# A decoder step on one core: the first norm, the last norm and two conditioning products are rearranged

## The chip, the core and the metric

One Trainium2 chip, one of its cores. The core has a matrix engine (TensorE, PE in the profile), a vector engine (VectorE, DVE), an activation engine (ScalarE, ACT), a general engine (GpSimd, POOL) and a sequencer that mostly issues transfers (SyncE, SP). Sixteen DMA engines carry all transfers. The metric is the device time of one execution in microseconds (us); lower is better. The inputs are float32; the kernel splits each large operand into a float32r high part and a float32r remainder ("hi" and "lo") and forms a product from three passes, so that it stays near float32.

## The reference

`x` is 1024 prompt rows and 8 x 8 sample rows of 1024 features, 1088 columns in the kernel's layout (features on partitions, 8 row blocks of 128 features). Cut to what the change touches:

```python
sh, sc, gt = ada_mod(c, w_ada_mix, b_ada_mix)        # silu(c) @ w + b, split in three
h = rms_norm(x, norm_mix) * (1 + sc) + sh            # the first norm
P = h @ w_in                                         # 34 column blocks of 128
...                                                  # RWKV-7 branch, pooling branch, merge
x = x + gt * (merged @ w_out)
sh, sc, gt = ada_mod(c, w_ada_mlp, b_ada_mlp)
h = rms_norm(x, norm_mlp) * (1 + sc) + sh
x = x + gt * (square(relu(h @ w_ff1)) @ w_ff2)
y = rms_norm(x, norm_final)                          # the last norm
```

`rms_norm` divides each row of `x` by the root of the mean of its squares. In the kernel's layout that mean runs across partitions.

## The kernel before, in words

**Order.** PE takes its instructions in the order of the program; the other engines' order is set by a scheduler from dependencies. Which piece of PE work comes next is decided while the program is written out: class `Pace` keeps a count of planned PE nanoseconds. A background generator (`back`) yields one product triple at a time; foreground generators yield either a number (planned nanoseconds until their next piece) or a condition. So a gap given in the code places a piece of work at a point of PE's order; if its data is late, PE stands still there.

**Start (`start`, L342 to L409).** Eight blocks `x` (544 KB each) are loaded over SP's queue, the sample columns once more as `smp` over ACT's queue (L350). Each block is squared on ACT (L362) and added up on DVE (L366). `stats` (L276) multiplies the sum with a column of ones, so that rows of `x` come to lie on partitions; root (L286), reciprocal (L287), a PE transpose of the broadcast result (L293) and a copy (L303) give `rb`, the reciprocal root on all partitions. The conditioning `silu(c) @ w_ada_mix` is done in parts of 1024 columns by `ada_part` (L239): four steps of two 512 KB tiles `aw`, PE work `wc<-aw,sT`, then a copy `asb` (L255), four small products that bring features back onto partitions (L259) and the bias (L263). Part 0 gives shift and scale of blocks 0 to 3, part 1 those of 4 to 7; part 2 (the gate) is done later in `ada_fill`. With them a block's row is made: `h` (L391, DVE), `hi` (L393, ACT), `lo` (L395, DVE), the sample columns by L386 to L388, L394 and L396.

**First products.** `phase1` (L1146) runs the column blocks J4 and J12 of `w_in` first, one row block of `h` at a time: for each of the eight rows, three column chunks of each of the two jobs, three passes each (18 products a row, 144 in all). Afterwards the other 32 jobs run, `weights` (L157) preparing each 128 x 512 half: load, `whi` on ACT (L167), `wlo` on DVE or POOL (L168).

**Middle (`phase2`, L1223).** Eight `or_job`s form the merged rows `t` (L1262, L1266 on POOL, hi and lo by L1269 and L1270), then `out_job(m, i)` multiplies them with `w_out`: eight `m` with two column chunks (i = 0), then eight with the third chunk (i = 1). The second conditioning, `ada` (L1238), runs beside them through `ada_part` with its tiles in the pool `hid`. Its first four tiles are passed through `behind` (L1233): POOL copies one column of the newest `t` at that point of the program into the tile, so that its load can't start before that `t` is there. The first step is placed 9000 + 6500 planned ns after job 4, the others 6500 apart.

**End.** `last` (L1401) multiplies the last group of `w_ff2` chunk by chunk over the column chunks `FCH` (L1506); `residual` (L1454, and L1457 with L1459 for sample columns) adds each block to `x`. `norm3` (L1422) follows a chunk behind: squares (L1431), sums (L1433), `stats` (L1436), `rms` (L1437), then eight rows out: one DVE instruction each (L1444), in the last chunk two of them on POOL and ACT (L1441, L1442), and a store on SP's queue (L1445).

Of the kernel before, what the change touches and what calls it, by code (L numbers as in the profile page):

```python
# [18 lines left out]
P = 128  # L19
# [98 lines left out]
class K:  # L118
# [38 lines left out]
    def weights(self, src):  # L157
# [10 lines left out]
        (nc.gpsimd if n % 2 and n >= self.solo else nc.vector).tensor_tensor(lo, raw, hi.bitcast(F32), op=ALU.subtract)  # L168
# [112 lines left out]
    def rms(self, po, col, blocks, out):  # L281
# [5 lines left out]
        nc.vector.reciprocal(r, r)  # L287
        yield 2000
        for i in range(0, k, 4):
            m = min(4, k - i)  # L290
            ps = self.ps("wc")
# [50 lines left out]
    def start(self, st, order):  # L342
# [4 lines left out]
        aw = lambda: st.tile([P, 1024], F32, tag="aw", bufs=8, name=self.nm("aw"))  # L347
        asb = st.tile([P, 512], F32, name="asb")
        smp = st.tile([P, 8, 64], F32, name="smp")
        nc.scalar.dma_start(smp, io["xT"][:, :, NPR:NT].rearrange("k p n -> p k n"))  # L350
        blocks = self.blocks(0, NT)
        po = self.ps("w")
        rt = self.cp.tile([P, 16], F32, tag="rt", bufs=2, name=self.nm("rt"))
        nc.scalar.activation(rt[:, 0:1], self.eps[:, 0:1], AF.Sqrt)
        xs = []
        t = None
        for kb in range(8):
            x = self.row(st, "x", 8)
            nc.sync.dma_start(x, io["xT"][kb])
            xs.append(x)  # L360
            sq = self.row(st, "sq", 3)
            nc.scalar.activation(sq, x, AF.Square)  # L362
            if t is None:
                t = sq
            else:
                nc.vector.tensor_tensor(t, t, sq, op=ALU.add)  # L366
        ws = []

        def load(i):
            for k in range(8):  # L370
                ws.append(aw())
                nc.sync.dma_start(ws[-1], io["w_ada_mix"][k, i])
# [3 lines left out]
        self.stats(po, t, blocks, True, True)  # L376
        rb = self.row(st, "rb", 1)
        pr, sa = slice(0, NPR), slice(NPR, NT)

        def part(i, gaps, turn):  # L380
            yield from self.ada_part("w_ada_mix", i, lambda: ws.pop(0), asb, self.am, "b_mix", (4 * i, 8 + 4 * i), gaps, turn)
            self.mod_scale(g, self.am, "norm_mix", 4 * i, 4 * i + 4)
            ks = slice(4 * i, 4 * i + 4)
            seq = lambda t: t[:, ks, 1:9].unsqueeze(3).to_broadcast([P, 4, 8, 8])
            s4 = smp[:, ks].rearrange("p k (q t) -> p k q t", t=TS)
            nc.vector.tensor_tensor(smp[:, ks], smp[:, ks], rb[:, sa].unsqueeze(1).to_broadcast([P, 4, 64]), op=ALU.mult)  # L386
            nc.vector.tensor_tensor(s4, s4, seq(g), op=ALU.mult)
            nc.vector.tensor_tensor(s4, s4, seq(self.am), op=ALU.add)  # L388
            for kb in range(4 * i, 4 * i + 4):
                x, h, hi, lo, sh = xs[kb], self.row(st, "h", 2)[:, pr], self.hh[kb], self.hl[kb], self.am[:, kb, 0:1]  # L390
                nc.vector.scalar_tensor_tensor(h, x[:, pr], g[:, kb, 0:1], rb[:, pr], op0=ALU.mult, op1=ALU.mult)  # L391

                nc.scalar.activation(hi[:, pr], h, AF.Identity, bias=sh)  # L393
                nc.scalar.activation(hi[:, sa], smp[:, kb], AF.Copy)  # L394
                nc.vector.scalar_tensor_tensor(lo[:, pr], h, sh, hi[:, pr].bitcast(F32), op0=ALU.add, op1=ALU.subtract)  # L395
                nc.vector.tensor_tensor(lo[:, sa], smp[:, kb], hi[:, sa].bitcast(F32), op=ALU.subtract)  # L396

        self.pace.run(iter(()), [part(0, (0, 3500, 0, 0), 1000), self.rms(po, 0, blocks, rb)])
        load(1)

        def rest():
            yield from part(1, (0, 0, 3000, 1500), 1500)
            self.done.add("h")
# [65 lines left out]
    def pool_cols(self, g):  # L469
# [4 lines left out]
        def begin():  # L474
# [3 lines left out]
            nc.sync.dma_start(ev[:, :, 0:15], self.io["spool"][:, g])  # L478
# [46 lines left out]
    def pools(self):  # L525
# [3 lines left out]
        for g in range(4):  # L529
            plw = self.pxp.tile([P, P], F32, tag="plw", bufs=1, name=self.nm("plw"))  # L530
            nc.sync.dma_start(plw, self.io["pool_w"][:, g * 128:(g + 1) * 128])
# [691 lines left out]
    def phase2(self):  # L1223
# [14 lines left out]
        def ada():  # L1238
# [183 lines left out]
        def norm3():  # L1422
            rb = T()
            for ci, (c0, n) in enumerate(FCH):
# [3 lines left out]
                for m in range(8):  # L1428
# [9 lines left out]
                for m in (7, 6, 0, 1, 2, 3, 4, 5):  # L1438
                    x = self.xr[m][:, c0:c0 + n]
                    if m > 5 and ci == 2:  # L1440
                        nc.gpsimd.tensor_tensor(x, x, rb[:, c0:c0 + n], op=ALU.mult)  # L1441
                        nc.scalar.activation(x, x, AF.Copy, scale=self.par("norm_final", m))  # L1442
                    else:
                        nc.vector.scalar_tensor_tensor(x, x, self.par("norm_final", m), rb[:, c0:c0 + n], op0=ALU.mult, op1=ALU.mult)  # L1444
                    nc.sync.dma_start(io["o_y"][m][:, c0:c0 + n], x)  # L1445
# [60 lines left out]
FCH = [(0, 448), (448, 384), (832, 256)]  # L1506
# [71 lines left out]
```

## Time and profile before

| what | value |
|---|---|
| time, median of 3 runs | 1757.21 us (1755.92 to 1760.8) |
| the profiled execution: its time / its span | 1759.32 us / 1757.5 us |
| mean granted clock of PE in it | 0.984 |
| PE busy | 1692.8 us, 96% of the span |
| DVE / ACT / POOL busy | 845.0 / 546.1 / 255.1 us |
| DMA | 179.61 MB, mean 102 GB/s |

Rows of the timeline read: start (us from the span's start), length, engine, line, operation, output <- inputs, shape, count, and in brackets how long the engine had stood still before it and what ended that. Rows of the waits read: the waiting engine and line, what it waited for, us in total, times, longest. Windows give a stretch, its length, the busy time and the instructions of PE, PEld, DVE, ACT and POOL, the granted PE clock, the busy share of the DMA engines and GB/s. The span leaves out 1.8 us of the profiled execution's time.

### The profile page before, as it was taken

How to read it: one execution, taken by the hardware profiler on the slowest of the kernel's cores; microseconds unless marked ns; L12 is line 12 of the kernel's file. 1: busy time of each engine (PE TensorE's matmuls, PEld its weight loads, DVE VectorE, ACT ScalarE, POOL GpSimd, SP SyncE). 2: the span in 40 equal slices, each digit the busy share in tenths (PEclk: the TensorE clock that was granted, in tenths of full speed). 3: DMA queues.
4: the chain of work that ended last, by engine and by line, in shares of the span. 5: the costliest groups of instructions: out<-in, count | busy, mean ns of one | idle time of the engine just before them, and what ended most of it. 6: DMA issues, size and time to landing. Idle time of an engine off the chain costs nothing.

```text
span 1757.5 us, 32572 instructions
## 1 busy us (share of the span) xinstructions
PE 1692.8 (96%) x13705; PEld 1583.7 (90%) x13705; DVE 845.0 (48%) x1540; ACT 546.1 (31%) x1100; POOL 255.1 (15%) x335
## 2 busy tenths in 40 slices
PE   5999999999999999999999999999999999999997
PEld 2989878887888798899798999999999999999997
DVE  5577465746573744335437633323333333324346
ACT  4443343343343433322225521213121212212132
POOL 0120110000000000005314411111111111111111
PEclk9999999989999999999999999999999999999998
DMA  8233314222413241847842311111111111111112
GB/s 336 82 128 118 125 65 135 85 81 94 147 41 129 80 137 57 314 168 276 299 151 85 136 45 49 43 44 47 43 46 45 43 49 43 43 49 43 43 43 103
DMA packets 80083, 179.61 MB, mean 102 GB/s; under 512 B 16480, under 2 KB 23136, under 8 KB 79936
## 3 DMA queue, kind: packets, MB, share of 16 engines
q1 hardware_dynamic: 72128, 156.66, 26.0%
q10 hardware_dynamic: 6512, 15.96, 2.7%
q0 software_dynamic: 1296, 4.90, 0.7%
q8 instruction: 108, 1.77, 0.4%
q14 instruction: 39, 0.32, 0.1%
HBM read 138.64 MB, written 38.84 MB: 101 GB/s over the span
## 4 chain that ended last, share of the span: by engine, by line
PE 86%; DMA 4%; DVE 4%; ACT 2%; issue 2%; POOL 1%; SPq 0%; DVEq 0%; ACTq 0%; POOLq 0%
PE mm L148 58%; PE w L148 24%; PE wc L148 4%; DMA t<-d_th 1%; DMA smp<-in_xT 1%; PE w L155 1%; POOL t L1266 1%; DMA aw<-in_w_ada_mix 1%; DMA wraw<-in_w_in 1%; DMA hid<-in_w_ada_mlp 0%; ACT whi L167 0%; DVE hx L1444 0%; DMA wraw<-in_w_ff 0%; POOL wlo L168 0%; DVE wlo L168 0%
## 5 line engine op out<-in xcount | busy, mean ns | idle before, releaser
L148 PE MATMUL mm<-hx,whi 128*128 128x362 f32 (+2 forms) x2608 | 683.1, 344 | 2.6 <-ACT px L465 2.0
L148 PEld LDWEIGHTS mm<-hx,whi 128*128 128x128 f32 x2608 | 458.8, 191 | 39.6 <-issue 20.4
L148 PE MATMUL mm<-hx,wlo 128*128 128x362 f32 (+3 forms) x1304 | 430.7, 330 | 1.8 <-DVE wlo L168 1.8
L167 ACT ACTIVATE whi<-wraw 128x512 fp32r<-128x512 f32 x246 | 155.1, 630 | 531.4 <-PE w L148 359.1
L148 PE MATMUL mm<-ma,whi 128*128 128x364 f32 (+1 forms) x1280 | 318.0, 330 | 0.2 <-ACT whi L167 0.2
L148 PEld LDWEIGHTS mm<-hx,wlo 128*128 128x128 f32 x1304 | 249.9, 192 | 2.3 <-DVE wlo L168 2.1
L148 PEld LDWEIGHTS mm<-ma,whi 128*128 128x128 f32 x1280 | 226.7, 189 | 7.3 <-issue 5.0
L168 POOL TENSOR_TENSOR wlo<-wraw,whi 128x512 fp32r<-128x512 f32 x89 | 117.6, 1322 | 670.4 <-ACT whi L167 670.4
L168 DVE TENSOR_TENSOR wlo<-wraw,whi 128x512 fp32r<-128x512 f32 x157 | 110.4, 704 | 211.6 <-ACT whi L167 211.3
L148 PE MATMUL mm<-ma,wlo 128*128 128x364 f32 (+1 forms) x640 | 210.4, 329 | 0.1
L1454 DVE SCALAR_TENSOR_TENSOR hx<-mm,aq,hx 128x364 f32<-128x364 f32 (+4 forms) x136 | 74.8, 588 | 207.8 <-PE mm L148 207.5
L148 PE MATMUL w<-mb,whi 128*128 128x362 f32 x640 | 159.1, 330 | 2.5 <-DVE rs L1457 2.1
L148 PEld LDWEIGHTS mm<-ma,wlo 128*128 128x128 f32 x640 | 120.6, 189 | 0.4 <-DVE wlo L168 0.4
L148 PEld LDWEIGHTS w<-mb,whi 128*128 128x128 f32 x640 | 112.7, 189 | 5.9 <-issue 4.4
L1349 DVE TENSOR_TENSOR ft<-ft 128x362 f32<-128x362 f32 (+1 forms) x96 | 53.1, 577 | 131.5 <-ACT ft L1348 131.2
L148 PE MATMUL w<-mb,wlo 128*128 128x362 f32 x320 | 105.5, 330 | 0.8 <-DVE wlo L168 0.8
L148 PE MATMUL w<-hx,whi 128*128 128x362 f32 x416 | 103.2, 329 | 0.1
L148 PE MATMUL mm<-hid,whi 128*128 128x364 f32 (+4 forms) x304 | 75.0, 328 | 0.0
L148 PEld LDWEIGHTS w<-hx,whi 128*128 128x128 f32 x416 | 73.7, 190 | 0.4 <-DVE hx L396 0.4
L1348 ACT ACTIVATE ft<-mm 128x364 f32<-128x364 f32 x64 | 29.5, 475 | 124.9 <-PE mm L148 124.7
L148 PE MATMUL w<-hx,wlo 128*128 128x362 f32 x208 | 67.8, 326 | 0.0
L1459 POOL TENSOR_TENSOR hx<-hx,rs 128x64 f32<-128x64 f32 x72 | 38.6, 537 | 176.8 <-DVE rs L1457 176.6
(309 smaller groups left out, 2120.8 us busy)
## 6 DMA issues: line engine op xcount, KB each, us to landing
wraw<-in_w_ff SPq DMA_DIRECT2D x134, 256.0 KB, 2.6
wraw<-in_w_in SPq DMA_DIRECT2D x68, 256.0 KB, 2.8
hid<-in_w_ada_mlp SPq DMA_DIRECT2D x24, 512.0 KB, 4.8
d_th<-px SPq DMA_DIRECT2D x22, 544.0 KB, 3.0
wt<-d_x SPq DMA_DIRECT2D x20, 544.0 KB, 4.4
t<-d_th ACTq DMA_DIRECT2D x16, 544.0 KB, 5.7
aw<-in_w_ada_mix SPq DMA_DIRECT2D x16, 512.0 KB, 7.2
wraw<-in_w_out SPq DMA_DIRECT2D x32, 256.0 KB, 2.9
```

Of the source, the lines that this page charges most:

```text
L148: return self.nc.tensor.matmul(out, lhsT, rhs, **kw)
L155: self.nc.tensor.transpose(out, in_, ident)
L167: nc.scalar.activation(hi, raw, AF.Copy)
L168: (nc.gpsimd if n % 2 and n >= self.solo else nc.vector).tensor_tensor(lo, raw, hi.bitcast(F32), op=ALU.subtract)
L1266: nc.gpsimd.tensor_tensor(t, t, S["u"], op=ALU.add)
L1348: nc.scalar.activation(t[:, :n], ps[:, :n], AF.Relu)
L1349: nc.vector.tensor_tensor(t[:, :n], t[:, :n], t[:, :n], op=ALU.mult)
L1454: nc.vector.scalar_tensor_tensor(x[:, c0:c0 + m], ps[:, :m], gt[:, 0:1], x[:, c0:c0 + m], op0=ALU.mult, op1=ALU.add)
L1459: nc.gpsimd.tensor_tensor(x[:, NPR:NT], x[:, NPR:NT], t, op=ALU.add)
```

## The change

**Start.** The squares are summed in three groups (blocks 0 to 2, 3 to 5, 6 and 7), and each group's sum is multiplied with a 128 x 128 tile of ones, accumulating in three PSUM tiles; so the sum stands on all partitions at once. Root (ACT), a transpose of 32 x 32 blocks (DVE), the reciprocal of one column of each block, and a second transpose of its broadcast give `rb`. `smp` goes over POOL's queue and its arithmetic to POOL. The conditioning is done in quarters (two row blocks each) of two 1 MB tiles, loaded in pieces of 256 columns (1 KB), by `load(qi)`, `round_(qi, r)` and `vectors(qi, wait)`; `rows(qi)` makes the two rows in cuts, with a single `h` tile. The first two `wlo` go to POOL. Two small loads of the pooling branch (`spool`, `pool_w`) go from SP's queue to POOL's.

**Middle.** `ada` is placed at 13000 + 6200 planned ns, further steps 6200 apart. `out_job(m, 1)` alternates between PSUM tags `w` and `mm`.

**End.** `FCH` is turned round, so that the sample columns lie in the first chunk and the last chunk is columns 0 to 255. Of the middle chunk's eight rows, 0 to 3 go to POOL and ACT, 4 and 5 are held until the last residual (through a copy of it into the tile `nf` that holds their scale), 6 and 7 until the last reciprocal. The last chunk's six DVE rows read the transposed reciprocal from PSUM; odd rows are stored over ACT's queue.

```diff
-        (nc.gpsimd if n % 2 and n >= self.solo else nc.vector).tensor_tensor(lo, raw, hi.bitcast(F32), op=ALU.subtract)
+        (nc.gpsimd if n < 2 or n % 2 and n >= self.solo else nc.vector).tensor_tensor(lo, raw, hi.bitcast(F32), op=ALU.subtract)
...
-        nc.scalar.dma_start(smp, io["xT"][:, :, NPR:NT].rearrange("k p n -> p k n"))
+        nc.gpsimd.dma_start(smp, io["xT"][:, :, NPR:NT].rearrange("k p n -> p k n"))
...
+            if kb in (2, 5, 7):
+                for s, ps in zip(parts, pss):
+                    self.mm(ps[:, :s.stop - s.start], ones, ts[-1][:, s], start=kb == 2, stop=kb == 7)
...
-        def load(i):
-            for k in range(8):
-                ws.append(aw())
-                nc.sync.dma_start(ws[-1], io["w_ada_mix"][k, i])
+        def load(qi):
+            for r in range(2):
+                w = st.tile([P, 2, 4, 256], F32, tag="aw", bufs=5, name=self.nm("aw"))
+                for s in range(2):
+                    o = s * 512 + qi % 2 * 256
+                    nc.sync.dma_start(w[:, s], io["w_ada_mix"][4 * r:4 * r + 4, qi // 2, :, o:o + 256].rearrange("k p c -> p k c"))
+                ws.append(w)
         load(0)
         back = self.stream(None, order)
+        load(1)
+        for s, ps in zip(parts, pss):
+            n = s.stop - s.start
+            nc.scalar.activation(rb[:, s], ps[:, :n], AF.Sqrt, bias=self.eps[:, 0:1], scale=1.0 / D)
+            nc.vector.transpose(rt1[:, s], rb[:, s])
+            c = slice(s.start // 32, s.stop // 32)
+            nc.vector.reciprocal(rr[:, c], cut32(rt1)[:, c, 0])
+            nc.vector.transpose(cut32(rb)[:, c, :], rr[:, c].unsqueeze(2).to_broadcast([P, n // 32, 32]))
...
+            for kb in (2 * qi, 2 * qi + 1):
+                x, h, hi, lo, sh = xs[kb], self.row(st, "h", 1, w=NPR), self.hh[kb], self.hl[kb], self.am[:, kb, 0:1]
+                cuts = [slice(a, min(a + n, NPR)) for a, n in CH] if kb < 2 else [slice(0, 512), slice(512, NPR)]
...
-            yield from part(1, (0, 0, 3000, 1500), 1500)
+            for qi in range(1, 4):
+                yield (0, 1500, 1800)[qi - 1]
+                round_(qi, 0)
+                yield (0, 500, 700)[qi - 1]
+                round_(qi, 1)
+                yield from vectors(qi, 1100)
+                rows(qi)
...
-                yield from self.ada_part("w_ada_mlp", g, tile, asb, self.aq, "b_mlp", (8 * g, 8 * g + 4), 6500, 2500, 9000 if g == 0 else 0)
+                yield from self.ada_part("w_ada_mlp", g, tile, asb, self.aq, "b_mlp", (8 * g, 8 * g + 4), 6200, 2500, 13000 if g == 0 else 0)
...
-                       (("mm", "mm"), ("w",))[i], lambda: self.done.add(("out", m, i)), lambda: mg)
+                       (("mm", "mm"), (("w", "mm")[m % 2],))[i], lambda: self.done.add(("out", m, i)), lambda: mg)
...
+                if ci == 2:
+                    nc.gpsimd.tensor_copy(nf[:, 4:5], self.xr[7][:, c0:c0 + 1])
+                    nc.gpsimd.tensor_copy(nf[:, 4:6], self.part[:, PC["norm_final"] + 4:PC["norm_final"] + 6])
+                    for o in late[:2]:
+                        o()
                 yield from self.rms(po, 0, bl, rb[:, c0:c0 + n])
...
+                else:
+                    nc.vector.tensor_copy(nf[:, 6:7], self.rt[:, 0:1])
+                    nc.vector.tensor_copy(nf[:, 6:8], self.part[:, PC["norm_final"] + 6:PC["norm_final"] + 8])
+                    for o in late[2:]:
+                        o()
+                    for m in (7, 6, 0, 1, 2, 3, 4, 5):
+                        out(m, rb[:, c0:c0 + n] if m > 5 else self.rps[:, :n], m > 5)
...
-FCH = [(0, 448), (448, 384), (832, 256)]
+FCH = [(640, 448), (256, 384), (0, 256)]
```

More of the change, by code (lines that the diff above doesn't have):

```diff
@@ L287, in rms @@
         nc.vector.reciprocal(r, r)
+        self.rt = r
         yield 2000
@@ L403, in rest @@
+        for r in range(2):
+            round_(0, r)
+        for _ in vectors(0, 0):
+            pass
+        rows(0)
+        load(2)
+        load(3)
+        def rest():
+            for qi in range(1, 4):
[5 more added lines that the diff above has]
+                rows(qi)
             self.done.add("h")
@@ L1423, in norm3 @@
             rb = T()
+            nf = self.cp.tile([P, 8], F32, name="nf")
             for ci, (c0, n) in enumerate(FCH):
```

101 lines of the change are left out of this document (60 added, 41 removed).

## The prediction, made before the changed kernel was run

> **What bounds the kernel now.** I read the busy slices first, then PE's waits, then the stretches where PE stands still.
>
> ```profile
> PE   5999999999999999999999999999999999999997
> ```
> ```profile
> PE w L148 <- DVE sq L366: 19.0, 1, 19.0
> PE wc L148 <- DVE t L1433: 3.7, 2, 2.9
> PE wc L148 <- DMA hid<-in_w_ada_mlp: 3.4, 2, 2.0
> PE w L148 <- DVE rs L1457: 2.1, 1, 2.1
> ```
>
> PE is full but in the first and the last slice (44 us each). PE's order is fixed by the program, so time saved in the first slice is passed on to the end. The change touches four of the waits: the start, the last norm, one transfer in the middle, one PSUM buffer. The start, by the timeline (PE's rows and one each of SP and ACT), with SP's waits behind it:
>
> ```profile
> 15.95 4.22 SPq L372 DMA_DIRECT2D aw<-in_w_ada_mix  x8
> 16.19 1.11 ACT L362 ACTIVATE sq<-x 128x1088 f32<-128x1088 f32 x1 [0.28 <-DVE sq L366]
> ...
> 36.82 1.05 PE L148 MATMUL wc<-aw,sT 128*32 128x512 f32 x4 [0.21 <-DMA aw<-in_w_ada_mix]
> 37.80 0.95 PE L148 MATMUL mm<-hx,whi 128*128 128x364 f32 x2
> ...
> 41.67 1.06 PE L148 MATMUL wc<-aw,sT 128*32 128x512 f32 x8
> ...
> 46.94 0.96 PE L148 MATMUL wc<-kct,asb 128*128 128x18 f32 x8
> ...
> 56.10 0.44 PE L148 MATMUL mm<-hx,wlo 128*128 128x364 f32 x1 [1.83 <-DVE wlo L168]
> ...
> 68.90 0.50 PE L148 MATMUL mm<-hx,whi 128*128 128x362 f32 x2
> ...
> 69.40 0.49 PE L148 MATMUL mm<-hx,whi 128*128 128x364 f32 x2
> ```
> ```profile
> SPq L372 <- DMA smp<-in_xT: 10.3, 1, 10.3
> ```
>
> The first product comes at 37.8, right behind conditioning work that waited for its weights; J4 and J12 end at 69.4, where the next job's first chunk starts. The conditioning weights are issued only at 15.95, because SP stood 10.3 us for the small `smp` transfer. A triple of passes takes 0.50 us, so the 144 products take 24.0 us.
>
> **The start, worked out.** What the transfers do:
>
> ```profile
> 11.00:14.00 3.00, 0.00 (x0) 0.00 (x0) 2.79 (x3) 2.51 (x3) 0.00 (x0) 1.00 1.03 411
> 15.50:18.00 2.50, 0.00 (x0) 0.00 (x0) 2.29 (x3) 2.20 (x3) 0.00 (x0) 1.00 0.44 121
> 1753.00:1754.00 1.00, 0.00 (x0) 0.00 (x0) 0.68 (x2) 0.00 (x0) 0.00 (x0) 0.50 0.78 263
> ```
> ```profile
> x<-in_xT SPq DMA_DIRECT2D x8, 544.0 KB, 8.7
> smp<-in_xT ACTq DMA_DIRECT2D x1, 256.0 KB, 14.7
> ```
>
> The engines move 411 GB/s until the inputs are in (about 15.4) and then fall to 121. With `smp` off SP's way the weights are issued behind `x` at about 6 and the gap closes. Their pieces shrink from 4 KB to 1 KB. No row shows such loads; the nearest is the last rows' stores, also 1 KB pieces: 263 GB/s at a busy share of 0.78, so 337 when full. The ends are 411 (no loss) and 263; I take 340, the row with the same piece.
>
> Before the first product PE's new order holds all four steps of quarters 0 and 1: 4.2 MB, and 0.5 MB of `w_in` between them. They are in at 15.4 + 4.2/0.34 + 0.5/0.4 = 29.0; the last step takes 1.05 (rows 36.82, 41.67), so the first product comes at 30.4 with some latency. Is the norm ready by then?
>
> ```profile
> L758 DVE STREAM_TRANSPOSE iv<-iv x8: 1048/1052/1073, 142.9 to 651.2; 128x512 f32<-128x512 f32 x8
> L148 PE MATMUL wc<-aw,sT x64: 592/593/1062, 22.9 to 44.8; 128*32 128x512 f32 x64
> ```
>
> The last square is split and summed by 17.3. Each ones product of 512 columns is two instructions like the second row, whose slow form is 1.06: 2.1 at worst, so the last group is done by about 20. Four wide transposes of 1.05 and the small ones make 5.3 on DVE: `rb` stands at about 25. Quarter 0's conditioning is through PE at 22.7, its vectors at about 25; two rows of DVE work (four passes of 1.28, row L395 below) then take 5.3, the first cut 1 us. So the norm is hidden behind the weights by about 4 us; if that cover went, every us beyond it would count in full.
>
> From the first product: 24.0 of products, four more steps of 1.05, three groups of small products of 0.96, and again a wait of about 1 for a `wlo` that DVE has queued behind rows (1.83 before): 32.1, ending at 62.5 to 62.7. The last quarter, 4.2 MB more, lands at about 42 to 43, just where PE wants it after 6.7 us of products. So 69.4 becomes 62.7: **6.7 us less** (nothing with 263 GB/s, by the sum of the slower rival below; 9 with 411). The single `h` tile costs nothing: `h` and `lo` of a row are both DVE's, and DVE needs about 6 us for two rows where PE has 8.5.
>
> ```profile
> L395 DVE SCALAR_TENSOR_TENSOR hx<-h,am,hx x8: 1278/1279/1284, 37.0 to 59.2; 128x1024 fp32r<-128x1024 f32 x8
> 854.04 2.25 DVE L168 TENSOR_TENSOR wlo<-wraw,whi 128x512 fp32r<-128x512 f32 x1 [0.68 <-ACT whi L167]
> ```
>
> The second row is a `wlo` beside a POOL sum: 2.25. POOL's new work, about 2.2 us for two rows, may so cost DVE 1.5 us for two rows; the 2.5 us of slack cover it. The Trainium skill (GPSIMD Engine Reference, Specifications) speaks against this part of the change: POOL shares its SBUF interfaces with VectorE and contends with instructions of two SBUF inputs, which the row passes are. The trace agrees by that row's 2.25; the sum would change only if the slack went.
>
> **The middle.** What the wait on `hid` hangs on:
>
> ```profile
> 846.79 1.05 PE L148 MATMUL wc<-hid,sT 128*32 128x512 f32 x4 [2.04 <-DMA hid<-in_w_ada_mlp]
> ...
> 849.34 0.30 POOL L1235 COPY hid<-t 128x1 f32<-128x1 f32 x2
> 849.36 0.49 PE L148 MATMUL mm<-ma,whi 128*128 128x364 f32 x2
> ...
> 852.93 2.81 POOL L1266 TENSOR_TENSOR t<-t,t 128x1088 f32<-128x1088 f32 x1
> ...
> 857.44 0.53 DVE L1270 TENSOR_TENSOR mb<-t,mb 128x362 fp32r<-128x362 f32 x1
> ```
>
> The first step moves from 15.5 to 19.2 planned us after job 4; jobs 5 to 7 take 36 products each, 17.8 in all. So it passes from within job 7 to behind it: its wait of 2.04 goes. But the next two tiles are then marked with job 7's `t` (added until 855.74), no more with job 6's (the copies at 849.34). Their loads start about 6 us later, and SP's weight loads wait behind them; they land near 860 to 861.5, while PE comes to the second step at about 857 to 858. Before that, PE, 4 us earlier, meets row 7 of the merged data, whose `lo` is made at 857.44. So the stall changes its name: I take **0.5 us more** (2 less if the sum comes sooner with PE ahead, 3 more if the loads are slow). What hangs on `ada`'s end has 10 us to spare (its last small products at 910, the sums of `x` at 922).
>
> ```profile
> 910.30 0.96 PE L148 MATMUL wc<-kct,asb 128*128 128x18 f32 x8
> ...
> 922.14 1.39 PE L148 MATMUL wc<-kct,t 128*128 128x6 f32 x12
> ...
> 951.48 0.57 PE L148 MATMUL w<-mb,whi 128*128 128x362 f32 x2 [2.07 <-DVE rs L1457]
> ...
> 961.51 0.43 PE L148 MATMUL w<-mb,wlo 128*128 128x362 f32 x1 [0.82 <-DVE wlo L168]
> ```
> ```profile
> 940.00:960.00 20.00, 17.59 (x103) 16.73 (x101) 20.00 (x27) 12.65 (x20) 10.01 (x7) 1.00 0.28 91
> ```
>
> Alternating PSUM tags take away the 2.07. But DVE is full from 940 to 960, and the next `wlo` comes from it: PE gets there earlier and waits there. I take nothing (2 less at best). The two small loads on POOL's queue are issued beside PE's full stretches: nothing.
>
> **The end.** PE's last product, DVE, and what follows:
>
> ```profile
> 1738.70 4.33 DVE L1444 SCALAR_TENSOR_TENSOR hx<-hx,part,t 128x384 f32<-128x384 f32 x8
> ...
> 1742.92 0.87 PE L148 MATMUL mm<-hx,ma 128*128 128x256 f32 x6
> ...
> 1744.20 0.73 DVE L1454 SCALAR_TENSOR_TENSOR hx<-mm,aq,hx 128x192 f32<-128x192 f32 x2
> ...
> 1746.66 1.86 PE L148 MATMUL wc<-kct,t 128*128 128x2 f32 x8 [2.87 <-DVE t L1433]
> 1748.57 0.26 ACT L286 ACTIVATE rt<-wc,eps 128x2 f32<-128x2 f32 x1 [1.89 <-PE wc L148]
> ...
> 1750.28 3.40 DVE L1444 SCALAR_TENSOR_TENSOR hx<-hx,part,t 128x256 f32<-128x256 f32 x6 [1.26 <-ACT t L303]
> ```
>
> Products end at T = 1743.8. The eight rows of the middle chunk hold up DVE until 1743.0, so residuals and sums run until 1746.6; the last row ends at T+9.9, the span at T+13.7. After: residual to T+0.6, square 1.05, the second set of sums on PE (0.5 to 0.9) to T+2.0, root 0.26 and reciprocal to T+2.5, two copies and two held rows (0.54 each) to T+3.9, six rows of 0.45 to 0.57 to T+6.9. That is **3.0 us less** (2 to 4), with 3.8 behind it as before. The stores, 0.8 MB of held rows and 1.05 MB of last rows, end by T+8.6 at 337 GB/s, no later than the last row's own store. The held rows 4 and 5 fill DVE's wait for the root; if they came late, the reciprocal would wait up to 1.1.
>
> **Sum.** -6.7 + 0.5 - 3.0 = -9.2 against the profiled execution: span 1757.5 to 1748.3, time 1759.32 to 1750.1. That execution lay 2.1 above the median 1757.2, so the median to come is **1748.0**.
>
> **The rivals.**
> - *Small pieces cost nothing, and the middle's stall goes too.* All weights at 411: first product 28.3, start -9, middle -2, end -3.5: 1742.7. The Trainium skill (DMA: Bandwidth & Descriptors, Specifications) gives 512 B as the least transfer for line rate, by which this is so. The trace rather speaks against it: 263 GB/s at share 0.78 for 1 KB beside 411 at 1.03.
> - *Half of the start or more is lost*: pieces at 263 to 300 GB/s, or SP held by another transfer until 16 again (3 us of idle DMA): start 0 to -3.5, rest as above: 1751.2 to 1754.7.
> - *A wait takes the place of the one removed*: the marked tiles cost 3 in the middle, and the held rows stand ahead of the reciprocal, so that the end gives 2: 1751.5, on the border.
> - *Slower*: the quartered weights are the bound. PE's order puts all of them before the end of its third row; the end of J4 and J12 is their landing plus 1.05 + 1.1 + 0.96 + 17.3 + 1. At R GB/s they land at 16.7 + 8400/R. With 248 GB/s the gains of the end are just eaten; at 200 they land at 58.7, J12 ends at 80, the whole is 8 slower: 1765. `smp`, in 256 B pieces, took 14.7 us for 0.26 MB; against it speak the 263 at share 0.78.
> - *The change doesn't do what it says*: SP's wait passes to another transfer; this is the second rival's price.
>
> **Chances.** A measurement of this kernel tells about 0.3%, 5.3 us, from no change: faster is below 1751.9. The forecast (1744.5 to 1751.5) 0.55; small pieces free 0.18; half or more lost 0.12; a new wait 0.09, half of it on either side of the border; slower 0.06. So faster 0.78, same 0.16, slower 0.06. The range 1741 to 1755 leaves out the slower case and the fringes of the others.
>
> **What would show it.** SP's wait for `smp` gone and `aw` issued near 6; GB/s above 330 from 15 to 40; the first product near 30.4 behind a wait on `aw`; J12's end near 62.7; in the middle a wait on `hid` of about 3 behind job 7's sum; DVE free of L1444's successor while the last residuals run, and the last row some 7 us after the last product. I am wrong if the norm on DVE, not the weights, ends last before the first product, or if 1 KB pieces move below 300 GB/s.

## The result, and the profile after

The changed kernel is no faster: 1760.89 us (median of 18 runs, 1756.44 to 1767.34) beside 1756.49 us for the kernel before on the same chip (18 runs, 1753.38 to 1761.18). The ratio is 1.0023, with a 95% interval of 1.0012 to 1.0034: about 4 us slower where 9 us less was forecast. The interval lies above 1, but by the 0.3% that one measurement of this kernel can tell from no change the two are the same; the time lies above the forecast range. The profiled execution took 1762.42 us, with a span of 1760.6.

The slices first, then PE's waits (engine, line, waited for; us in total, times, longest):

```profile
PE   5999999999999999999999999999999999999997
```
```profile
PE mm L148 <- DVE sq L367: 13.5, 2, 11.6
...
PE wc L148 <- DMA hid<-in_w_ada_mlp: 2.8, 2, 1.8
PE wc L148 <- ACT asb L410: 2.6, 2, 1.8
...
PE wc L148 <- DMA aw<-in_w_ada_mix: 2.0, 1, 2.0
PE wc L148 <- DVE t L1486: 1.9, 2, 1.1
PE w L148 <- DVE wlo L168: 1.8, 1, 1.8
...
PE wc L148 <- issue: 0.8, 1, 0.8
```

The slices look as before. Of the four waits of the prediction the one on `sq` is 5.5 us shorter, the one on `t` 1.8 shorter, the one on `rs` is gone; in their place the waits on `asb` (2.6 for 1.2) and `aw` (2.0 for 0.4) have grown, while those on `wlo`, under two names, sum to 2.6 in both kernels. By this list the kernel should be faster; but PE's busy time went from 1692.8 to 1702.3 us for nearly the same products (13712 for 13705), so they run slower somewhere. The start by the timeline (ACT and SP, then PE):

```profile
5.32 10.42 SPq L381 DMA_DIRECT2D aw<-in_w_ada_mix  x4
...
17.59 6.88 PE L148 MATMUL mm<-sq,ones 128*128 128x512 f32 x12 [1.91 <-DVE sq L367]
...
17.79 1.29 ACT L365 ACTIVATE sq<-x 128x512 f32<-128x512 f32 x3 [0.26 <-DMA x<-in_xT]
...
31.25 1.93 PE L148 MATMUL wc<-aw,sT 128*32 128x512 f32 x8 [1.98 <-DMA aw<-in_w_ada_mix]
33.11 0.98 PE L148 MATMUL mm<-hx,whi 128*128 128x364 f32 x2
...
37.05 1.88 PE L148 MATMUL wc<-sel,asb 128*128 128x9 f32 x8 [1.76 <-ACT asb L410]
...
41.64 0.81 PE L148 MATMUL mm<-hx,whi 128*128 128x362 f32 x2
...
71.02 0.49 PE L148 MATMUL mm<-hx,whi 128*128 128x364 f32 x2
```

And the same stretch by windows (the granted clock is the third number from the end, then DMA share and GB/s):

```profile
30.00:35.00 5.00, 3.75 (x14) 1.94 (x14) 4.96 (x8) 1.82 (x4) 4.86 (x8) 0.51 1.10 348
35.00:40.00 5.00, 3.24 (x13) 2.95 (x13) 3.31 (x8) 2.00 (x4) 0.53 (x3) 0.50 1.10 353
40.00:45.00 5.00, 5.00 (x25) 3.08 (x27) 4.18 (x6) 1.45 (x2) 3.51 (x5) 0.63 0.80 266
```

The weights are issued at 5.32 and move at 348 GB/s, as forecast. But the last square starts at 17.79 (16.19 before; the prediction had the inputs in at 15.4), and from 30 to 43 PE has half its clock: a step of 8 takes 1.93 instead of 1.06, a pair of passes 0.81 instead of 0.49. The first product comes at 33.11 (forecast 30.4, before 37.80), J12's end at 71.02 (62.7, before 69.40). The end of the program is as forecast:

```profile
1749.73 0.48 DVE L1526 SCALAR_TENSOR_TENSOR hx<-mm,aq,hx 128x256 f32<-128x256 f32 x1 [0.28 <-PE mm L148]
...
1750.84 1.15 DVE L1503 SCALAR_TENSOR_TENSOR hx<-hx,nf,t 128x384 f32<-128x384 f32 x2
...
1752.20 0.17 DVE L287 RECIPROCAL rt<-rt 128x2 f32<-128x2 f32 x1 [0.21 <-ACT rt L286]
...
1753.85 2.44 DVE L1503 SCALAR_TENSOR_TENSOR hx<-hx,part,wc 128x256 f32<-128x256 f32 x6
```

PE's last product ends at T = 1749.69, the last row at T+6.6 (forecast T+6.9, before T+9.9). The span ends at T+10.9, where before had T+13.7.

To see where time goes between the two ends I matched PE's rows of two traces in their order and took the difference of their starts. In us, against the profile of before; each column is a time in before, and a plus is later:

| kernel | 69.5 | 183 | 204 | 293 | 494 | 680 | 745 | 820 | 1000 | 1742 | span end behind T |
|---|---|---|---|---|---|---|---|---|---|---|---|
| changed | +1.6 | +1.9 | +3.7 | +3.7 | +3.8 | +3.9 | +5.7 | +5.8 | +5.4 | +5.9 | 10.9 |
| changed, second profile (e14) | -2.7 | -2.4 | -0.5 | +1.2 | -0.4 | -2.0 | +0.1 | +0.1 | +5.1 | +5.6 | 11.0 |
| before, second profile (e13) | -0.2 | -0.1 | -0.1 | -1.6 | -3.3 | -3.3 | -3.1 | -3.1 | +2.2 | +2.2 | 12.9 |
| e1_tail | 0.0 | 0.0 | 0.0 | -1.5 | -3.3 | -3.2 | -1.5 | -1.4 | +0.4 | +0.4 | 10.7 |
| e2_start | +1.6 | +1.5 | +3.5 | +2.1 | +0.5 | +0.5 | +0.1 | +0.1 | +2.0 | +2.1 | 13.0 |
| e3_warm | -2.4 | -2.2 | +1.3 | +1.3 | -3.4 | -3.4 | -1.1 | -1.0 | +7.6 | +8.2 | 10.9 |
| e4_nosmall | -4.9 | -4.8 | -3.7 | -3.7 | -4.3 | -4.2 | -2.3 | -2.2 | -0.4 | +0.1 | 10.8 |
| e6_oldhid | -3.3 | -3.3 | -2.2 | -3.6 | -6.8 | -8.4 | -6.5 | -6.4 | -3.7 | -3.6 | 10.8 |
| e10_wlo_dve | -4.0 | -3.9 | -1.9 | -1.9 | -4.8 | -6.4 | -6.1 | -6.0 | -5.1 | -5.1 | 10.7 |
| e9_mid | -0.2 | -0.3 | -0.3 | -1.8 | -3.3 | -3.2 | -1.1 | -1.1 | +2.6 | +3.2 | 13.3 |
| e16_hid | -0.2 | -0.2 | -0.2 | -0.1 | -0.2 | -0.2 | -0.4 | -0.4 | +3.7 | +4.2 | 12.7 |

The table is read by the steps in a row, not by its last column: the change has effects at 0 to 70, at 183 to 204, at 820 to 1000 and behind 1742; the steps between 204 and 820 appear in two profiles of the same kernel too (before against itself: up to 3.3). In the six profiles that are not listed the step from 820 to 1000 is +0.5 to +4.9, and the reference is a lucky one there: before's first profile has no lost clock from 760 to 1000 (its second 5.1 us; lost clock is one minus the granted clock, summed over time).

### The profile page after: what moved, and what is told of

It is laid out like the page before. It is cut to its first block, busy times and chain, and to the rows that moved or that the text cites. A ratio compares the mean times of both kernels' runs of the same rounds, so it can differ in the third digit from the quotient of the medians.

```text
span 1760.6 us, 32648 instructions
## 1 busy us (share of the span) xinstructions
PE 1702.3 (97%) x13712; PEld 1590.2 (90%) x13712; DVE 843.5 (48%) x1554; ACT 549.6 (31%) x1108; POOL 281.9 (16%) x379
## 4 chain that ended last, share of the span: by engine, by line
PE 87%; DVE 5%; DMA 3%; ACT 2%; issue 2%; POOL 1%; SPq 0%; DVEq 0%; ACTq 0%; POOLq 0%
PE mm L148 58%; PE w L148 24%; PE wc L148 4%; DMA t<-d_th 1%; PE w L155 1%; POOL t L1318 1%; DMA x<-in_xT 1%; DVE t L1377 0%; DVE wlo L168 0%; DMA hid<-in_w_ada_mlp 0%; DVE ma L1379 0%; DVE h L432 0%; DVE bk L664 0%; DVE d L496 0%; DVE t L1486 0%
## 5 line engine op out<-in xcount | busy, mean ns | idle before, releaser
L1526 DVE SCALAR_TENSOR_TENSOR hx<-mm,aq,hx 128x364 f32<-128x364 f32 (+3 forms) x136 | 75.0, 588 | 206.2 <-PE mm L148 206.1
L148 PE MATMUL w<-mb,whi 128*128 128x362 f32 x576 | 143.8, 331 | 0.0
L148 PEld LDWEIGHTS w<-mb,whi 128*128 128x128 f32 x576 | 102.6, 191 | 2.5 <-issue 1.7
L148 PE MATMUL w<-mb,wlo 128*128 128x362 f32 x288 | 95.5, 332 | 1.8 <-DVE wlo L168 1.8
```

The source lines that it names most:

```text
L148: return self.nc.tensor.matmul(out, lhsT, rhs, **kw)
L1526: nc.vector.scalar_tensor_tensor(x[:, c0:c0 + m], ps[:, :m], gt[:, 0:1], x[:, c0:c0 + m], op0=ALU.mult, op1=ALU.add)
```

## The experiments

Times are medians; ratios are against the kernel before on the same chip. Theory: PE's half clock, the late `x` rows and POOL's work beside DVE's rows ate the start, and the middle cost little. Rivals: the middle's edits; the norm or the weights as the start's bound.

**e1_tail: the end alone.** The kernel before with `norm3`, `rms` and `FCH` of the change.

```diff
+                    late = [] if ci == 0 else [lambda m=m, out=out, r=rb[:, c0:c0 + n]: out(m, r) for m in range(4, 8)]
...
-FCH = [(0, 448), (448, 384), (832, 256)]
+FCH = [(640, 448), (256, 384), (0, 256)]
```

> The kernel before with the last norm's edits alone (the held rows, the copies nf, rms from PSUM, the order of the last chunks). Theory: the end was read rightly, and its gain of about 2.8 us stands by itself: span 1754.5 to 1755, ratio 0.998 to 0.999, the last DVE row ending some 6.6 us after the last product, first product and J12's end as before (37.8, 69.4). Rival: the gain of the end is bought by work that the held rows push elsewhere, and the ratio is 1.000.

Span 1754.9; 1756.30 us, ratio 0.9997 (0.9988 to 1.0006). The last row ends at T+6.6. The end works alone as it does in the whole, but the ratio shows less than the profile. Everything up to the last products is in the same order as in before, and yet PE's offset went to -3.3 and back to +0.4: the first sign of chance.

**e15_tail_again: the same once more.** No edit against e1_tail.

> e1_tail once more (the kernel before with the end's edits alone). Theory (the end gains 2.9 us in every execution, and the ratio of 0.9997 was the low end of chance): ratio 0.998 to 0.9995, end of span 10.9 us behind the last product. Rival (something in the end's edits takes the gain back in most executions): ratio at 0.9995 to 1.0005 again.

Span 1751.2; 1753.94 us, 0.9992 (0.9979 to 1.0005). Both intervals hold 1 to 2 us of gain. The profiles give 2.3 us: in six profiles with the old end the span ends 12.7 to 13.7 behind T (mean 13.1), in the others near 10.8. The first profile of before was the longest of the six, so its 13.7 flattered the forecast. Why the ratios show a little less than 2.3 stays open.

**e2_start: the start alone** (with the first two `wlo` and the small loads on POOL). Its edit is the whole start of the change; two lines of it:

```diff
-        nc.scalar.dma_start(smp, io["xT"][:, :, NPR:NT].rearrange("k p n -> p k n"))
+        nc.gpsimd.dma_start(smp, io["xT"][:, :, NPR:NT].rearrange("k p n -> p k n"))
...
-            nc.sync.dma_start(plw, self.io["pool_w"][:, g * 128:(g + 1) * 128])
+            nc.gpsimd.dma_start(plw, self.io["pool_w"][:, g * 128:(g + 1) * 128])
```

> The kernel before with the start's edits alone (ones product, transposing norm, quartered weights, single h tile, first two wlo on POOL, small loads on POOL's queue); middle and end as before. Theory: the start itself is no gain but a loss of about 1.6 us at J12's end (71.0 for 69.4), and what follows adds 1 to 4 us of shifted half-clock spells and instruction waits: ratio 1.002 to 1.004, PE clock near 0.5 between 30 and 43 us. Rival 1 (the middle's edits make the loss): ratio 1.000 or below. Rival 2 (the two profiles differ by chance in the start): first product near 30 and ratio below 0.998.

Span 1758.9; 1758.72 us, 1.0012 (1.0001 to 1.0023). The start repeats to 0.1 us (J12's end +1.6), and a step of 2.0 at 183 to 204 is there too. By the ratio the start by itself costs 2.1 us (0.2 to 4.0).

**e3_warm: dummy products in PE's pauses.** They compute nothing that is used.

```diff
+        def dummy(n):
+            for _ in range(n):
+                nc.tensor.matmul(warm, ones, xs[0][:, :512], start=True, stop=True)
         for r in range(2):
             round_(0, r)
+        dummy(1)
...
                 round_(qi, 0)
+                if qi == 1:
+                    dummy(2)
```

> The changed kernel with three dummy ones products on PE whose results nobody reads: one behind the second step of quarter 0, two between the steps of quarter 1, where PE stood still at 29.3 to 31.2. Theory (PE's half clock costs the start about 4.5 us): the granted clock stays at 1.0 from 30 to 43, a triple takes 0.5 instead of 0.9, J12 ends at 66 to 67.5 instead of 71.0, and the whole is 3 to 5 us faster than the changed kernel. Rival (DVE's and ACT's rows set the pace, the slow clock only fills their waits): J12 ends within 1 us of 71 at full clock, with longer waits on h and lo instead.

J12's end is 4.0 us earlier than in the changed kernel. The windows of e3_warm:

```profile
30.00:35.00 5.00, 3.95 (x21) 1.79 (x20) 4.80 (x10) 2.89 (x6) 1.96 (x4) 1.00 1.10 348
35.00:40.00 5.00, 5.00 (x26) 3.13 (x25) 4.18 (x7) 1.44 (x2) 3.56 (x6) 0.67 1.10 354
```

So at full clock the start is as much shorter as the theory said, and DVE's rows were not the pace. That the dummies did all of it is not shown: the twelve ones products, which stand ahead of them, took 4.09 us here instead of 6.88, and the changed kernel's own second profile (e14, below), without dummies, ended J12 4.3 us earlier than its first. For the dummies speaks that the three kernels that have them (e3, e7, e12) show a granted clock of 1.00 from 24 to 36 us, and none of the eight profiles with the new start and without dummies does. But the whole was no faster: 1761.51 us, 1.0029 (1.0017 to 1.0041). The 2.4 us that it had on the kernel before were gone at 204, and between 820 and 1000 it lost 8.6. The theory for the whole had a hole: the middle.

**e4_nosmall: nothing small beside `x`.** `smp` is made by POOL from the `x` rows; `spool` and `pool_w` go back to SP.

```diff
-        nc.gpsimd.dma_start(smp, io["xT"][:, :, NPR:NT].rearrange("k p n -> p k n"))
...
+            for kb in (2 * qi, 2 * qi + 1):
+                nc.gpsimd.tensor_tensor(smp[:, kb], xs[kb][:, sa], rb[:, sa], op=ALU.mult)
```

> The changed kernel without small transfers beside x: smp is no longer loaded but made by POOL from the sample columns of the x rows that are on the chip anyway, and spool and pool_w are issued on SP as before. Theory: the x rows land sooner, the last square starts at 15.4 to 16.2 instead of 17.8, the norm is 1.5 to 2 us earlier, the weights about 1 us earlier, J12 ends at 69 to 70. Rival (the small pieces cost nothing, the 2 us are the x rows' own): last square at 17.5 to 18, J12 at 71 or later for the extra POOL work.

Better than expected: the last square starts at 15.52, J12 ends at 64.5.

```profile
15.52 1.29 ACT L364 ACTIVATE sq<-x 128x512 f32<-128x512 f32 x3 [0.25 <-DMA x<-in_xT]
```

Besides 2.3 us of landing time PE's ones products come closer together, and the half clock lasts from 25 to 32 only. Five more profiles without these loads (e5, e6, e7, e10, e12) have the last square at 15.5 to 16.0. Still 1756.68 us, 1.0006 (0.9994 to 1.0017): again lost in the middle.

**e11_smp_only: only `smp` is not loaded**, the other two stay on POOL's queue (e4's first edit alone).

> The changed kernel with one edit: smp is not loaded, but made by POOL from the sample columns of the x rows; spool and pool_w stay on POOL's queue. Theory (smp's 256 B pieces alone slow the x rows): last square at 15.4 to 16 instead of 17.8, J12's end near that of e4_nosmall (64.5), ratio 1.000 to 1.001. Rival (spool's small pieces, on POOL's queue at the same time, are as much to blame): last square at 16.5 to 17.5.

```profile
16.49 1.30 ACT L364 ACTIVATE sq<-x 128x512 f32<-128x512 f32 x3 [0.27 <-DMA x<-in_xT]
```

16.49: taking `smp` away gives the `x` rows 1.3 us, taking the other two away as well another 0.5 to 1.0. The price of `smp` is one beside the other two: alone on POOL's queue (e8_smp_queue, next) it leaves the last square at 16.29, where before, with `smp` on ACT's queue, has 16.19. The theory (15.4 to 16) fell; the rival's range begins where the result lies. 1757.58 us, 1.0007 (0.9994 to 1.0020).

**e8_smp_queue: the kernel before, `smp` on POOL's queue, nothing else.**

```diff
-        nc.scalar.dma_start(smp, io["xT"][:, :, NPR:NT].rearrange("k p n -> p k n"))
+        nc.gpsimd.dma_start(smp, io["xT"][:, :, NPR:NT].rearrange("k p n -> p k n"))
```

> The kernel before with one edit: smp is loaded by POOL's queue and no longer by ACT's, so that SP need not wait 10.3 us for it. Theory (SP's stand alone was worth the 3 us in which the transfers fell to 121 GB/s, the x rows pay some of it back to smp's small pieces): weights issued near 6, first product 0 to 3 us earlier, J12's end at 67 to 69.4. Rival (the wait passes to another transfer, or the norm on PE and DVE sets the first product): first product at 37 to 38 as before.

```profile
5.61 10.93 SPq L372 DMA_DIRECT2D aw<-in_w_ada_mix  x8
...
37.17 0.43 PE L148 MATMUL mm<-hx,whi 128*128 128x364 f32 x1 [1.52 <-ACT hx L393]
```

The weights are issued 10.3 us earlier, and the first product comes 0.6 us earlier, J12's end 0.3 later: PE now waits for the first row, its high part and then its low part. In the kernel before the weights and the norm ended together. 1756.82 us, 1.0011 (1.0000 to 1.0021): the rival was right.

**e5_oldmid and e6_oldhid: e4_nosmall with the middle of before**, e5 with both edits undone, e6 with the conditioning's times alone.

```diff
-... "b_mlp", (8 * g, 8 * g + 4), 6200, 2500, 13000 if g == 0 else 0)
+... "b_mlp", (8 * g, 8 * g + 4), 6500, 2500, 9000 if g == 0 else 0)
...
-                       (("mm", "mm"), (("w", "mm")[m % 2],))[i], lambda: self.done.add(("out", m, i)), lambda: mg)
+                       (("mm", "mm"), ("w",))[i], lambda: self.done.add(("out", m, i)), lambda: mg)
```

> The changed kernel without small transfers beside x (as in e4_nosmall) and with the gates' conditioning and the out jobs' PSUM tags of before. Theory (the later conditioning of the gates gives the start's gain back: in e4_nosmall PE lost 3 us on the kernel before between 845 and 975, behind hid, ma and wlo): no wait on ma, the loss there falls to 1 us or less, and the offset of -2 to -4 us reaches the end, where 2.9 more come: span 1751 to 1753.5, ratio 0.997 to 0.9985. Rival (whoever comes early waits there, whatever the middle's edits): the loss stays near 3 us and the ratio at 1.000 to 1.001.

> As e5_oldmid, but with the out jobs' alternating PSUM tags of the changed kernel: only the times of the gates' conditioning are those of before. Theory (the loss comes from the conditioning, not from the tags): as e5_oldmid within 1 us. Rival (the tags move the wait to wlo, 2.7 us in e4_nosmall for 0.8 before, and so cost as much): 1 to 2 us of loss at 955 to 975 remain.

1753.84 us, 0.9992 (0.9982 to 1.0003), and 1753.40 us, 0.9987 (0.9978 to 0.9996): by the ratios some 3 us better than e4_nosmall, and the tags make no difference. But the single profiles still lose 3.4 and 2.8 between 820 and 1000, more than e4's 1.8: where the single profile and the time part, the middle is not settled by them.

**e9_mid and e16_hid: the middle alone**, on the kernel before: both edits, then the conditioning's times alone (the first line pair of the diff above, reversed).

> The kernel before with the two edits of the middle alone: the gates' conditioning later, and the out jobs' alternating PSUM tags. Theory (the stretch from 800 to 860 is full of transfers, and PE waits for them under one name or another): the offset on the kernel before stays within 1 us between 845 and 1000, ratio 0.999 to 1.001. Rival (the later conditioning itself costs, as the 10 us lost there in e3_warm suggest): 3 us or more lost there, with waits on ma and hid, ratio 1.002 or more.

> The kernel before with the gates' later conditioning alone, the tags as before. Theory (the later conditioning makes e9_mid's loss): ratio 1.001 to 1.003, 3 us or more lost between 845 and 900, with waits on ma and hid. Rival (the tags make it): ratio 0.9995 to 1.0005.

1758.75 us, 1.0019 (1.0009 to 1.0028), and 1759.47 us, 1.0020 (1.0009 to 1.0032). So the later conditioning by itself costs 3.5 us (1.6 to 5.6), and the tags nothing. My own theory for e9 (nothing is lost) fell. PE in e16_hid:

```profile
846.80 1.07 PE L148 MATMUL wc<-hid,sT 128*32 128x512 f32 x8
...
854.98 0.43 PE L148 MATMUL mm<-ma,whi 128*128 128x364 f32 x1 [1.93 <-ACT ma L1269]
855.93 0.67 PE L148 MATMUL mm<-ma,whi 128*128 128x364 f32 x1 [0.52 <-DVE ma L1270]
...
858.72 1.92 PE L148 MATMUL wc<-hid,sT 128*32 128x512 f32 x4
861.50 1.92 PE L148 MATMUL wc<-hid,sT 128*32 128x512 f32 x4 [0.86 <-DMA hid<-in_w_ada_mlp]
```
```profile
850.00:860.00 10.00, 7.56 (x32) 5.47 (x30) 6.74 (x9) 3.41 (x6) 6.10 (x8) 0.77 0.78 278
860.00:870.00 10.00, 9.14 (x40) 6.87 (x39) 0.69 (x1) 0.63 (x1) 0.00 (x0) 0.72 0.60 231
```

And before, its second wait on `hid` and the same windows:

```profile
856.83 1.05 PE L148 MATMUL wc<-hid,sT 128*32 128x512 f32 x4 [1.35 <-DMA hid<-in_w_ada_mlp]
```
```profile
850.00:860.00 10.00, 8.65 (x49) 6.70 (x48) 6.97 (x8) 2.76 (x6) 6.10 (x5) 1.00 0.96 355
860.00:870.00 10.00, 10.00 (x63) 8.93 (x62) 2.05 (x4) 2.08 (x3) 1.28 (x1) 1.00 0.73 281
```

The waits are 1.93 + 0.52 + 0.86 = 3.3, as long as before's two on `hid` (2.04 + 1.35 = 3.4), only now on `ma` first. But behind them the clock drops: 0.77 and 0.72 in the two windows, which in before's first profile stood at 1.00. At half clock four products of a step take 1.92 instead of 1.05.

**e7_oldmid_warm and e12_oldhid_warm: e5 and e6 with three dummy products** (one ahead of quarter 1's first step, two behind it).

> e5_oldmid with three dummy ones products on PE (one ahead of the first step of quarter 1, two behind it), whose results nobody reads. Theory (PE's clock is worth what a busy PE keeps): granted clock 1.0 from 25 to 31 us where e4_nosmall had 0.5, J12's end 1 to 2 us before that of e5_oldmid (near 63 for 64.5), the rest as e5_oldmid: span 1749.5 to 1752. Rival (rows on DVE set the pace by then): J12's end within 0.5 us of e5_oldmid.

> e6_oldhid with the three dummy ones products of e7_oldmid_warm, whose results nobody reads. Theory: all that was found put together; granted clock 1.0 from 25 to 35, J12's end at 64 to 64.5 (5 us before the kernel before), 2 to 4 us of it lost in the middle, the end's 2.9 on top: ratio 0.997 to 0.9985. Rival: ratio 0.9985 to 0.9995, as the clock spells further on take the rest.

The start is as expected: J12's end at -5.1 and -5.3, at full clock from 25 to 72. The whole is not: 1754.45 us, 0.9988 (0.9978 to 0.9998), and 1756.18 us, 1.0001 (0.9991 to 1.0011). What they have on e5 and e6 at 70 us (2 us) is not found in the time, and e4_nosmall, with the same start and no dummies, had -4.9 there as well.

**e10_wlo_dve: e6_oldhid with the first two `wlo` on DVE.**

```diff
-        (nc.gpsimd if n < 2 or n % 2 and n >= self.solo else nc.vector).tensor_tensor(lo, ...)
+        (nc.gpsimd if n % 2 and n >= self.solo else nc.vector).tensor_tensor(lo, ...)
```

> e6_oldhid with the first two wlo on VectorE again instead of POOL. Theory (POOL's wlo slow the row passes beside them: three lo cuts took 3.62 us in e6_oldhid beside them and 1.66 without): these cuts take about 1.7, each wlo 0.6 to 1.1 on DVE, row 1 is 0.5 to 1 us earlier, the wait on asb shrinks, J12's end 0 to 1 us earlier. Rival (what DVE takes over costs as much as the contention): J12's end within 0.5 us or later.

Three `lo` cuts of row 0 on DVE, in e6_oldhid and then in e10_wlo_dve:

```profile
26.69 3.62 DVE L434 SCALAR_TENSOR_TENSOR hx<-h,am,hx 128x364 fp32r<-128x364 f32 x3
```
```profile
26.64 1.82 DVE L434 SCALAR_TENSOR_TENSOR hx<-h,am,hx 128x364 fp32r<-128x364 f32 x3
```

POOL's two `wlo` cost DVE 1.8 us here; made on DVE itself they take 1.43 us, most of it in a stretch in which it had nothing to do. J12's end is 0.7 earlier, which shows nothing: the three profiles with e6's start (e4, e5, e6) lie 1.9 apart there. 1753.95 us, 0.9987 (0.9976 to 0.9998).

**e13_before_again, e14_after_again: the two kernels once more**, unchanged.

> The kernel before once more, unchanged. Theory (chance in spells of half clock makes the differences between 240 and 800): a second profile of the same kernel is 0 to 3 us off the first there, with another count of spells, and equal to it within 0.1 us from 72 to 204 and at the end. Rival (each kernel has its own spells): equal within 0.5 us everywhere.

> The changed kernel once more, unchanged. Theory: the start repeats (last square near 17.8, half clock from 30 to 43, J12 near 71), the PE wait for nothing shown near 197 repeats, the offset at 745 differs by up to 3 us from the first profile, and where PE comes earlier at 845 it loses more there. Rival (the first profile's start was chance): J12 below 68.

1757.51 us, 1.0004 (0.9992 to 1.0016), and 1759.29 us, 1.0024 (1.0010 to 1.0039). Before differs from itself by up to 3.3 us between 204 and 820 and by 5.2 from 820 to 1000; the changed kernel's start by 4.3, because the half clock lasted from about 27 to 34 in the second profile (0.75 and 0.57 in two windows) and from 30 to 43 in the first. The forecast for its J12 (near 71) was wrong; that it loses in the middle when it comes early (+5.0 from 820 to 1000) was right.

## Why the prediction was wrong, step by step

**What bounds the kernel.** "Time saved in the first slice is passed on to the end" failed. In the seven profiles without the load of `smp` J12 ends 3.0 to 5.3 us early and the end of the program gains 2.3 more, and yet by their times none of these kernels is more than 2.3 us ahead of before. One place where it goes is clear: near 196 PE stands still for what the waits call `issue`, in the eleven profiles with the new start and in none of the seven with the old one; with the slow products behind it that is the step of 1.1 to 3.5 us between 183 and 204. How much the middle takes back because PE comes early is not settled: every profile but the changed kernel's first loses against before's between 820 and 1000, e2_start, which is not early there, as well (1.9). The changed kernel, then e3_warm:

```profile
196.06 1.06 PE L148 MATMUL wc<-wt,sT 128*32 128x512 f32 x6
197.89 1.02 PE L148 MATMUL wc<-wt,sT 128*32 128x512 f32 x2 [0.77 <-issue]
```
```profile
193.99 1.94 PE L148 MATMUL wc<-wt,sT 128*32 128x512 f32 x8 [2.00 <-issue]
```

Three dummies, six PE instructions, move the pause six products forward in the program. So it hangs on the place in PE's instruction stream, behind some 190 tiny products of 32 x 32, and the traces show what it is: the supply of instructions. The profile has a DMA queue for them, with the same row in before and in the changed kernel (packets, MB, share):

```profile
q8 instruction: 108, 1.77, 0.4%
```

These are 108 packets of 16 KB. Numbered in order of time, PE's instructions (products, weight loads and those of its sequencer) are 27680 in the changed kernel, and 108 times 256 is 27648. In all 18 profiles, behind the first 40 us, PE has 58 standstills of over 0.3 us that are called `issue`. Each ends at an instruction whose number is 193 or 194 above a multiple of 256, 256 n, and 1.2 to 1.6 us after the n-th packet has landed. Near 196 n is 11: this packet lands 3.8 to 4.8 us after the tenth, and PE is through the tiny products before it can go on. The kernels with the old start come to that instruction 1.7 to 2.5 us after the landing, and do not wait.

**The start (forecast -6.7; +2.1 by the time of e2_start; J12's end +1.6 and -2.7 in two profiles).** The first product comes 2.7 us later than forecast in both profiles of the changed kernel (33.11 and 33.09 for 30.4), 2.3 us of it for the late `x` rows: in e4 the step ahead of it comes at 28.99 instead of 31.25. From there to J12's end the first takes 5.6 us more than the forecast 32.3, with the half clock until 43, the second 1.3 more, with the half clock until 34. Three terms were mis-sized. "Inputs in at 15.4": 17.8, for the small loads moved to POOL's queue run beside `x` (e4: 15.5; e11: 16.5). "A triple 0.50", and all products at that price: between 30 and 43 a triple took 0.9, and the two profiles with a shorter spell end J12 4.0 (e3) and 4.3 us (e14) earlier. "POOL may cost DVE 1.5, the slack covers it": the price was right (1.8, e10), the slack was not there, since the norm came level with the weights and not 4 us ahead; so `asb`, queued on ACT behind the slow rows, held PE 1.76. The rate of the weights (348 GB/s for 340), the wait of SP and the four steps ahead of the first product were right, and the rival in which 1 KB pieces cost nothing fell with that rate. Neither of the two signs of being wrong came: the weights ended last, and they moved at over 300 GB/s. The step that failed is the one that costed PE's work, 0.50 a triple and 1.05 a step, by durations from a stretch in which PE was busy and at full clock, and carried them into one in which PE waits between them; the standstill for instructions (1.8 us in the first profile's step at 196) is a term that the sum did not have.

The row for the slow clock is the first window of the changed kernel above, 0.51. The Trainium skill (TensorE: Matmul & The Clock Gate, Part 1: The HAM clock gate) has it so: PE's clock is half or full, falls after an idle window of about 3.4 us and rises after a busy one, and the window runs freely, so that it differs from run to run. The trace agrees in the last points: lost clock comes in portions of about 1.7, which is 3.4 at half, and at other places in each profile. It disagrees in the idle time: a pause of 2.03 was enough in the changed kernel.

```profile
711.17 0.60 PE L148 MATMUL mm<-hx,whi 128*128 128x362 f32 x2 [2.03 <-ACT px L517]
...
713.36 0.52 PE L148 MATMUL w<-at,z 64*64 64x64 f32 x4
```

The changed kernel, above, runs its groups of four tiny products at 0.52 two us behind that pause. Before has the same pause and stays at 0.33:

```profile
706.97 0.60 PE L148 MATMUL mm<-hx,whi 128*128 128x362 f32 x2 [2.03 <-ACT px L465]
...
709.12 0.33 PE L148 MATMUL w<-at,z 64*64 64x64 f32 x4
```

That is the chance in the table between 204 and 820.

**The middle (forecast +0.5, within -2 to +3; alone 1.0020, +3.5 us, 1.6 to 5.6).** The chain was right: the first step passes behind job 7, PE meets the last row's `ma`, the next tiles load late. So were the lengths: from 760 to 1000 PE stands still 8.8 us on average in the seven profiles with the later conditioning, 8.4 in the eleven with the old one. What was left out is the clock: lost clock there is 5.8 us against 2.0 on average (3.4 to 10.2 against 0 to 5.1). The step from 820 to 1000, over all profiles, has the same direction, +4.0 against +2.1, so the profiles show 1.9 of the 3.5 us, with much chance in each. In before's first profile the waits are two, of 2.0 and 1.4 us, 10 us apart, and the clock stays at 1.00; in its second they are 2.5 and 2.9, 4 us apart, and it is at half for 6.8 us; with the later conditioning there are three within 9 us. That the closeness brings the clock down is argued from this, not shown; the lost clock is measured. The first profile of the changed kernel hides this (-0.4): it came 5.8 us late, with the transfers ahead of it; its second shows it (+5.0). Alternating tags were rightly costed at nothing: `wlo` takes the place of `rs` (2.70 in e6_oldhid).

**The end (forecast -3.0; by the profiles -2.3 on average, -2.8 in the two compared).** Right in mechanism and size, step by step.

**The sum.** Parts alone: start +0.12%, middle +0.19%, end -0.03% and -0.08%; together about +0.25%, 4.4 us, beside +0.23% for the whole, each part with some 0.1% either way. My slower rival (the weights as bound at 200 to 248 GB/s) was not the cause: they moved at 348. None of the rivals had a slower PE in it.

**A version that came out below both** is the start without small loads, the old times of the gates' conditioning and the new end, e6_oldhid or e10_wlo_dve: 0.9987 of the kernel before, 2.3 us, and 6 us below the changed kernel. That is less than the 0.3% that one measurement can tell, though the intervals lie below 1.

## What to carry to other kernels

A pause of PE can have two prices, its length and a half clock behind it; when an edit moves waits, cost the work behind them at half clock as the slower case. Before a gain at the head of a program is passed on to its end, look for the next place where PE waits for something that does not move with it, its own instructions behind a run of tiny products included, and take a second profile of the same kernel to learn how far two executions differ without any change. Where one wait ends the idle time, ask how far behind it the next one stands: here moving one load's queue freed 10 us of SP and gained nothing.

## What the runs showed of the hardware that was not expected

- Half-clock spells are placed anew in each execution: two profiles of one kernel differed by 3.3 us between 204 and 820 with the same instructions in the same order.
- PE's instructions come in packets of 16 KB, 256 instructions each. PE waited 0.3 to 2.6 us for the next one at two places in every profile (near 354 and 687), at others in some, and at one (near 196) in all those with the new start and no other.
- Three small loads beside eight of 544 KB (0.26 MB in 256 B pieces, and two smaller ones in 60 B and 512 B pieces) let the last of these land 1.7 to 2.4 us later (17.6 to 17.8 for 15.4 to 15.9); the two smaller ones alone cost 0.5 to 1.0 (16.4), the first alone 0.3 to 0.8 (16.2).
- A 128x512 transpose of 32x32 blocks from and to SBUF took 0.67 to 0.71 us on DVE at the start, where 1.05 was taken from another line; the norm was not slow for it, but for late rows and for slow ones products (6.88 us for twelve, 4.09 in e3_warm; by their length at half clock, though the trace's clock column shows 1.00 there).
